# First stage of a decoder step: memory keys and values as plain fp32 products, and GpSimd's arithmetic given to VectorE and ScalarE

## The chip, the cores and the metric

The kernel runs on one core of a Trainium2 chip. The metric is the device time of one execution in microseconds (us), lower is better. A core has five engines, each with its own queue of instructions that it works off in order: TensorE (PE in the profile, its weight loads PEld), VectorE (DVE), ScalarE (ACT), GpSimd (POOL) and SyncE (SP, here only for transfers). They wait for each other by semaphores.

## The reference, cut to what matters

The reference is one inference step of a two-layer decoder over 256 prompt tokens and 8 x 8 sampled tokens, with 1024 features. Layer 0 is a state-space layer (S5), layer 1 latent attention; after each of them the tokens attend to 256 memory tokens and go through an MLP. What the change touches:

```python
def mem_kv(mem, g, w_k, w_v):          # once per layer; layer 0 is changed
    mn = rms_norm(mem, g)              # 256 memory rows x 1024
    k = mn @ w_k                       # 1024 x 1024, four heads of 256
    v = mn @ w_v
    return k, v                        # both are outputs too

def s5_mixer(u, a, dt, b, c, d_skip, w_glu, h0):   # layer 0, shortened
    # abar = exp(a dt); bbar = coef * b  (complex, 64 groups x 64 states)
    # state:  h[t] = abar h[t-1] + bbar u[t]   (per group of 16 channels)
    # output: y[t] = Re(c h[t]) + d_skip u[t]
    z = gelu(y) @ w_glu                # 1024 x 2048
    return z[..., :dm] * sigmoid(z[..., dm:])
```

## The kernel before, in words

**Stages.** The work goes stage by stage: the S5 layer with the memory keys and values of layer 0 beside it (to about 190 us), the GLU product (to about 266 us), the memory attention and MLP of layer 0, and then layer 1 in the same way. The change is in the first stage alone.

**Split products.** Products with weights are made in three parts (`mm3`, lines 194 to 198). A weight chunk of 128x1024 is loaded (`wraw`); ScalarE makes its rounded high part (`whi`, line 190), and VectorE or, for the chunk numbers in `POOL_LO`, GpSimd makes the rest (`wlo`, line 191). The other operand is split in the same way, into `mnh` and `mnl` for the memory rows. TensorE then multiplies high by high, high by low and low by high (L196, L197, L198). In the first stage there are two buffers each for raw, high and low parts, so that at most two loads are under way.

**Memory keys and values** (`mem_kv`). Eight blocks of 256 columns, four of keys and four of values; each takes two chunks of weights, and each chunk 8 x 3 products of 128x128 by 256. VectorE multiplies a block of keys with the row norms (`kt`, L565), TensorE transposes it (`kps`), and ScalarE copies it out.

**S5.** The input `xc` is multiplied with its norms into `xr` (four times, L781), transposed (`ups`) and kept as `U`. `state_side(hq)`, for the four quarters hq, makes for each half hh the products of B with powers of a: `rb` from QX (L862), `t1` from QY (L863), their sum (L864). These tiles are called `tq` in the profile and share three buffers (tag `tmp4`). TensorE transposes `rb` (`rps`), ScalarE copies it to `rt`, and TensorE makes the states of each chunk (`sps`, L877). `out_side(hq)` makes the products of C with powers: `ca` from X1 (L900), `ct` from Y1 (L901), their sum (L902); for hq = 2 the tile is called `hca`. `scan(f)`, for both halves f of the groups, carries the states over the chunks in VectorE steps `sc` and `H` (L938 to L944) and copies them to `HS` (L959, L961). `outputs(hq)` uses `HS`, `ca` and `U` for the outputs (`yps`, `ytp`), whose split goes into the GLU.

**Order.** The program is written stage by stage, but the order on each engine is set when it is built, by a scheduler that simulates the program's times (`schedule_with_timeline_sim`, L1776). So other work brings another order, on other engines too. On the chip each engine keeps that order.

Of the kernel before, what the change touches and what calls it, by code (L numbers as in the profile page):

```python
# [10 lines left out]
F32 = mybir.dt.float32  # L11
# [73 lines left out]
POOL_LO = (3, 5) + (101,) + (102,) + (103,)  # L85
# [3 lines left out]
class Trunk:  # L89
# [17 lines left out]
    # statistics over the partitions of several feature blocks  # L107
# [24 lines left out]
    def root_ahead(self, extra=None):  # L132
        """the summand of a root to come, as a root itself: the function's table is loaded ahead"""
        b = self.sm.tile([128, 1], F32, name="rb", bufs=2)
        with self.tc.issue_after(self.last_exp.ins):
            self.nc.scalar.activation(b, self.eps[:, 1:2] if extra is None else self.eps[:, 2:3], AF.Sqrt)
        return b

    def exp_ahead(self):
        """the function's table is loaded ahead"""  # L140
        b = self.sm.tile([128, 1], F32, name="rb", bufs=2)
        with self.tc.issue_after(self.gate.ins):
            self.nc.scalar.activation(b, self.eps[:, 2:3], AF.Exp)

    def root(self, ss, dim, extra=None, tag="r", bias=None):
        """sqrt(ss / dim + eps) (or + extra)"""
# [24 lines left out]
    def wtile(self, kind, dtype):  # L171
        """a buffer for weights; the pools take turns"""
# [5 lines left out]
    def load_chunk(self, srcs, cols):  # L178
        """srcs: list of (column slice or AP shaper, dram AP); returns hi, lo [128, cols]"""
# [13 lines left out]

    def mm3(self, ps, wh, wl, xh, xl, start, stop):
# [5 lines left out]
    def dense(self, W, KT, nb, xh, xl, evac, Gs, n=NT, pairs=None, then=None, korder=None):  # L200
        """W: dram [KT*128, nb*128]; xh, xl: k -> AP [128, n]; Gs: group sizes.
        pairs: second column offset (in columns) for a group made of two halves."""
# [3 lines left out]
        while b0 < nb:  # L206
# [5 lines left out]
            for k0 in ks:  # L212
# [10 lines left out]
                # with the last weights a block is finished before the next  # L223
# [17 lines left out]
    def update(self, y, rt, gpost, stat=True):  # L241
        """h += y / rt * gpost"""
# [12 lines left out]
    def update_scaled(self, y, rt, gpost, gpre, restore=True):  # L255
        """h += y / rt * gpost; the next input is the split of (rt h) gpre for the new h, and its
        root takes eps rt^2: the factor rt of a token goes with the token's norm"""
# [28 lines left out]
    def next_root(self):  # L286
        """the root of the input that update_scaled left, once it is needed"""
        st, ex = self.pending
        return self.root(self.stat_sum(st), D, extra=ex)
# [129 lines left out]
    def token_rows(self, row, name):  # L419
        """a row over the tokens [.., NT] by blocks of tokens: [128, 3]"""  # L420
# [5 lines left out]
    def h_to_tokens(self, s, rt):  # L426
        """the residual s / rt with the tokens on the partitions"""
# [12 lines left out]
    def finish(self, W, KT, fh, fl, y, gpost, ex):  # L440
        """the last product, norm and residual: the norm with the tokens on the partitions"""
# [55 lines left out]
    def mem_x(self, pool):  # L497
# [8 lines left out]
    def mem_root(self):  # L506
        """the norms of the rows of the memory: in the first layer they go with the products"""
# [15 lines left out]
    def mem_prepare(self, l, mp, x):  # L523
# [3 lines left out]
        for j in range(KD):  # L527
            ps = (self.ps_at if l else self.ps_mm).tile([128, 512], F32, name="mps", tag="at" if l else "mm")
            for i in range(2):
# [3 lines left out]
            nc.vector.scalar_tensor_tensor(xl[:, j, :], m, g(j), xh[:, j, :].bitcast(F32),  # L533
                                           op0=ALU.mult, op1=ALU.subtract)
        self.kt = mp.tile([128, KD, MT], F32, name="kt", tag="kt")

    def mem_kv(self, l, op, x):
        """in units: the keys (two blocks of features each), then the values (a head each)"""
# [5 lines left out]
        for g in range(8):  # L544
            W, c0 = (Wk, g * 256) if g < 4 else (Wv, (g - 4) * 256)
            ps = [self.ps_mm.tile([128, 512], F32, name="mm", tag="mm") for _ in range(2)]
            for k0 in range(0, KD, 4):
                hi, lo = self.load_chunk([(lambda t: t.rearrange("p (k c) -> p k c", c=256), W[:, k0:k0 + 4, c0:c0 + 256])], 1024)
# [40 lines left out]
    def s5(self, mkv):  # L589
        sp, close_sp = self.open("s5")  # L590
        mn, close_mn = self.open("memn0", side="right")
        mx = self.mem_x(mn)
# [43 lines left out]
    def s5_scan(self, sp, mkv, mx):  # L636
# [5 lines left out]
        # parameters, rows: group; the state index twice  # L642
# [15 lines left out]
        # B and C, rows: (real | imaginary part, group)  # L658
# [10 lines left out]
        # rows: (half of the features, chunk)  # L669
# [7 lines left out]
        # the gains of the layer's input go into B and the skip weights  # L677
        nc.gpsimd.tensor_mul(nat['b'][:, :K * N].rearrange("p (k n) -> p n k", k=K),
# [3 lines left out]
        nc.gpsimd.tensor_mul(dn, dn, gxn[:G])  # L682
# [22 lines left out]
        # r of the tokens, rows: (half of the features, chunk), columns: steps  # L705
# [23 lines left out]
        # coefficients  # L729
# [14 lines left out]
        # products with a power, rows: (real | imaginary part)  # L744
        #   state side, descending powers times the coefficient: re x (qr | qi) + im x (-qi | qr)
        #   output side, powers 1..8: re x (pr | -pi) + im x (-pi | -pr)
# [20 lines left out]
        for t, v in ((X1, PI), (Y1, PR)):  # L767
            nc.gpsimd.tensor_scalar(t[bot], v[bot], -1.0, None, op0=ALU.mult)
        self.mem_root()
        self.chunk = 100  # L770
        self.mem_gains(sp)
        # chunks: rows (step, channel), one block of columns per group
# [6 lines left out]
        for fb in range(4):  # L779
            xr = xp.tile([2 * NCH, 8, L, K], F32, name="xr", bufs=2)  # L780
            nc.gpsimd.tensor_mul(xr, xc[:, :, fb * 128:(fb + 1) * 128].rearrange("p s (g k) -> p g s k", k=K),  # L781
# [10 lines left out]
        # B and C, rows: the state index twice  # L792
# [30 lines left out]
        # a^8, a^16, .. a^128 by (half of the groups, state index), with the signs of the complex product  # L823
# [16 lines left out]
        # states at the start of each chunk (H) and after the last (F), rows: (half of the groups, state index)  # L840
# [15 lines left out]
        def state_side(hq):  # L856
            rt = self.xp.tile([128, 2, 8, 128], F32, name="rt", tag="xl" if hq % 2 else "xh", padded_shape=[128, 2, 10, 128])
            for hh in range(2):
# [4 lines left out]
                (V if hq < 2 else nc.gpsimd).tensor_mul(t1, b4(BI, gs), p4(QY, gs))  # L863
# [21 lines left out]
        def out_side(hq):  # L885
            ca = []
            E = nc.gpsimd
# [15 lines left out]
            # impulse responses, rows: input channel  # L903
# [20 lines left out]
        # states after each chunk: a scan by doubling, up and down, over 16 columns of groups  # L924
        def scan(f):
# [24 lines left out]
            # the states by (real | imaginary part, state index)  # L950
# [62 lines left out]
        if True:  # L1013
            # final states
# [43 lines left out]
    def kv_open(self, l, kvp):  # L1058
        """keys and values of the sample group, loaded ahead"""
# [29 lines left out]
    def mem_attention(self, l):  # L1089
# [8 lines left out]
        if True:  # L1098
# [35 lines left out]
            # the softmax scales of the rows: prompt tokens (two blocks), sample rows (head, sequence, step)  # L1134
# [10 lines left out]
            # sample group  # L1145
# [42 lines left out]
            # prompt group  # L1188
# [68 lines left out]
    def mlp(self, l):  # L1257
# [5 lines left out]
        with tc.tile_pool(name="mlp", bufs=1, reuse_waits="tile") as hp:  # L1263
            # y = r^2 y' with y' the product without r: the post norm takes y' with eps / r^4
# [32 lines left out]
    def mla(self, close_mn):  # L1297
# [7 lines left out]
        if True:  # L1305
# [23 lines left out]
            if True:  # L1329
# [15 lines left out]
                # latent and rotary key  # L1345
# [18 lines left out]
                # rotary key on both halves of the partitions  # L1364
# [32 lines left out]
                # queries  # L1397
# [21 lines left out]
                # the prompt group takes keys and values out of the latent, the sample group its queries into it  # L1419
# [71 lines left out]
                def values_of(half):  # L1491
                    """the values of four heads"""
# [287 lines left out]
```

## Time and profile before

| what | value |
|---|---|
| time, median of 3 runs | 1270.54 us (1269.88 to 1273.55) |
| span of the profiled execution, first to last instruction | 1267.7 us |
| TensorE busy, share of the span | 1136.2 us, 90% |
| VectorE busy | 774.2 us, 61% |
| ScalarE busy | 560.1 us, 44% |
| GpSimd busy | 269.4 us, 21% |
| chain that ended last, by engine | PE 73%, DVE 16%, DMA 3%, ACT 2%, POOL 2% |
| mean granted TensorE clock | 0.956 |

The times are of executions without a profile; the span is of one profiled execution, and the difference between it and the median is 2.8 us. The shares are means over the span. They hide that the stages have different limits, so the change has to be read from its own stage: the stretches and single rows below.

### The profile page before, as it was taken

How to read it: one execution, taken by the hardware profiler on the slowest of the kernel's cores; microseconds unless marked ns; L12 is line 12 of the kernel's file. 1: busy time of each engine (PE TensorE's matmuls, PEld its weight loads, DVE VectorE, ACT ScalarE, POOL GpSimd, SP SyncE). 2: the span in 40 equal slices, each digit the busy share in tenths (PEclk: the TensorE clock that was granted, in tenths of full speed). 3: DMA queues.
4: the chain of work that ended last, by engine and by line, in shares of the span. 5: the costliest groups of instructions: out<-in, count | busy, mean ns of one | idle time of the engine just before them, and what ended most of it. 6: DMA issues, size and time to landing. Idle time of an engine off the chain costs nothing.

```text
span 1267.7 us, 21389 instructions
## 1 busy us (share of the span) xinstructions
PE 1136.2 (90%) x8233; PEld 1030.5 (81%) x8233; DVE 774.2 (61%) x1253; ACT 560.1 (44%) x1006; POOL 269.4 (21%) x229
## 2 busy tenths in 40 slices
PE   3665579989998899999999999999899989999996
PEld 2564568988687899999988996559776989999996
DVE  5999994467447763355478586334953495435543
ACT  5434346444344453355356435223533455434531
POOL 3656430035003500000031034400620050000011
PEclk9877789999998999999999999998899989999998
DMA  7221446863733254444443554626454324544441
GB/s 148 75 92 46 103 72 170 296 247 128 271 130 119 74 182 150 136 156 157 151 150 111 167 179 142 201 71 249 151 199 167 116 84 134 165 150 150 149 138 55
DMA packets 151234, 184.86 MB, mean 146 GB/s; under 512 B 16719, under 2 KB 119388, under 8 KB 151068
## 3 DMA queue, kind: packets, MB, share of 16 engines
q1 hardware_dynamic: 141660, 174.84, 43.6%
q10 hardware_dynamic: 6976, 5.46, 1.4%
q0 software_dynamic: 2496, 3.20, 0.8%
q8 instruction: 65, 1.06, 0.3%
q14 instruction: 37, 0.30, 0.1%
HBM read 174.89 MB, written 6.21 MB: 143 GB/s over the span
## 4 chain that ended last, share of the span: by engine, by line
PE 73%; DVE 16%; DMA 3%; issue 2%; ACT 2%; POOL 2%; SPq 1%; POOLq 0%; DVEq 0%; ACTq 0%
PE mm L197 18%; PE mm L196 18%; PE mm L198 17%; DVE wlo L191 2%; PE kt L102 2%; PE sps L1159 2%; PE s L1639 2%; DVE sc L939 2%; DMA xc<-in_x_sample 1%; PE pov L1216 1%; PE ops L1174 1%; PE s L1680 1%; DVE H L944 1%; DVE xl L271 1%; PE pps L1194 1%
## 5 line engine op out<-in xcount | busy, mean ns | idle before, releaser
L191 DVE TENSOR_TENSOR wlo<-wraw,whi 128x1024 fp32r<-128x1024 f32 (+1 forms) x219 | 273.4, 1252 | 276.3 <-ACT whi L190 274.4
L190 ACT ACTIVATE whi<-wraw 128x1024 fp32r<-128x1024 f32 (+1 forms) x232 | 241.5, 1045 | 299.2 <-PE mm L197 250.1
L197 PE MATMUL mm<-xl,whi 128*128 128x320 f32 x944 | 295.9, 316 | 14.4 <-DVE xl L97 6.1
L196 PE MATMUL mm<-xh,whi 128*128 128x320 f32 x944 | 281.6, 318 | 8.4 <-ACT t_up L1272 3.7
L198 PE MATMUL mm<-xh,wlo 128*128 128x320 f32 x944 | 285.9, 313 | 1.9 <-DVE wlo L191 1.9
L197 PEld LDWEIGHTS mm<-xl,whi 128*128 128x128 f32 x944 | 181.0, 192 | 18.6 <-DVE xl L271 7.8
L196 PEld LDWEIGHTS mm<-xh,whi 128*128 128x128 f32 x944 | 176.5, 192 | 11.6 <-ACT t_up L1272 3.9
L198 PEld LDWEIGHTS mm<-xh,wlo 128*128 128x128 f32 x944 | 178.6, 192 | 2.3 <-DVE wlo L191 2.3
L196 PE MATMUL mm<-hh,whi 128*128 128x320 f32 x512 | 158.2, 309 | 0.0
L197 PE MATMUL mm<-hl,whi 128*128 128x320 f32 x512 | 158.0, 309 | 0.0
L198 PE MATMUL mm<-hh,wlo 128*128 128x320 f32 x512 | 157.1, 308 | 0.0
L191 POOL TENSOR_TENSOR wlo<-wraw,whi 128x1024 fp32r<-128x1024 f32 x13 | 32.4, 2493 | 304.7 <-ACT whi L190 216.7
L197 PEld LDWEIGHTS mm<-hl,whi 128*128 128x128 f32 x512 | 96.1, 188 | 0.0
L196 PEld LDWEIGHTS mm<-hh,whi 128*128 128x128 f32 x512 | 96.1, 188 | 0.0
L198 PEld LDWEIGHTS mm<-hh,wlo 128*128 128x128 f32 x512 | 95.9, 188 | 0.0
L118 POOL TENSOR_TENSOR sq<-sq 128x320 f32<-128x320 f32 x34 | 41.0, 1205 | 203.3 <-ACT sq L120 202.6
L248 POOL TENSOR_TENSOR t_up<-y,rr 128x320 f32<-128x320 f32 x6 | 7.5, 1258 | 218.3 <-DVE h L249 218.3
L102 PEld LDWEIGHTS kt<-ident,kn 128*128 128x128 f32 x256 | 30.1, 147 | 20.9 <-issue 5.8
L102 PE MATMUL kt<-ident,kn 128*128 128x128 f32 x256 | 39.2, 291 | 7.8 <-ACT ktb L1086 2.9
L102 PE MATMUL rps<-ident,tq 128*128 128x128 f32 x64 | 11.2, 324 | 37.1 <-DVE tq L864 26.1
L1568 POOL DMA_DIRECT2D rop<-in_cache_k_rope x64 | 34.4, 537 | 38.2 <-issue 20.5
L102 PEld LDWEIGHTS rps<-ident,tq 128*128 128x128 f32 x64 | 8.8, 167 | 37.8 <-issue 23.2
(483 smaller groups left out, 2171.4 us busy)
## 6 DMA issues: line engine op xcount, KB each, us to landing
wraw<-in_w_mlp_up SPq DMA_DIRECT2D x64, 512.0 KB, 3.9
wraw<-in_w_mlp_down SPq DMA_DIRECT2D x64, 512.0 KB, 3.6
kn<-in_cache_mem_k SPq DMA_DIRECT2D x16, 1024.0 KB, 7.6
vn<-in_cache_mem_v SPq DMA_DIRECT2D x16, 1024.0 KB, 9.4
wraw<-in_w_mem_k SPq DMA_DIRECT2D x16, 512.0 KB, 3.3
wraw<-in_w_mem_v SPq DMA_DIRECT2D x16, 512.0 KB, 3.8
wraw<-in_w_glu SPq DMA_DIRECT2D x32, 256.0 KB, 3.5
wraw<-in_w_mem_q SPq DMA_DIRECT2D x16, 512.0 KB, 4.0
```

The costliest lines, as they stand in the source:

```text
L102: self.nc.tensor.transpose(out, in_, self.ident[b:b + k, b:b + k])
L118: eng.tensor_add(st['acc'], st['acc'], st['last'])
L190: nc.scalar.activation(hi[:, :cols], raw[:, :cols], AF.Copy)
L191: (nc.gpsimd if self.chunk in POOL_LO else nc.vector).tensor_sub(lo[:, :cols], raw[:, :cols], hi[:, :cols].bitcast(F32))
L196: nc.tensor.matmul(ps, wh, xh, start=start, stop=False)
L197: nc.tensor.matmul(ps, wh, xl, start=False, stop=False)
L198: nc.tensor.matmul(ps, wl, xh, start=False, stop=stop)
L271: lo = nc.vector.scalar_tensor_tensor(xl[:, j, :], s, gpre(j), xh[:, j, :].bitcast(F32), op0=ALU.mult, op1=ALU.subtract)
L939: V.tensor_mul(m[1], swp, bc(a8i))
L1159: nc.tensor.matmul(sps[h * 32:(h + 1) * 32, :MT], qm[:, h * 2 + db, j * 128 + i * 32:j * 128 + (i + 1) * 32], ktb[:, h * 2 + db, :], start ...
L1568: last[eng] = eng.dma_start(dst, src[bass.ds(v, 1)].rearrange("o p d -> (o p) d"))
L1639: nc.tensor.matmul(s[o(b), :], ql(rb, b), lts[b][:, rb, :], start=rb == 0, stop=False, skip_group_check=True)
```

## The change

- The memory keys and values of layer 0 become plain fp32 products. The weights are not split; `load_plain` uses the six buffers of raw, high and low parts in turn, so that six loads may be under way. The memory rows are one tile, `mnp`, without a low part. A chunk takes 8 products in place of 24. Layer 1 keeps the split form.
- GpSimd's arithmetic in this stage goes to VectorE: the gains into B and into the skip weights (`natb`, `dn`), `xr`, `t1` of the quarters 2 and 3, and all of `out_side`.
- The negations for X1 and Y1 go from GpSimd to ScalarE.
- Comments are dropped, so that line numbers move by 22 or 23 in the functions below.

```diff
-POOL_LO = (3, 5) + (101,) + (102,) + (103,)
+POOL_LO = (3, 5)
...
+    def load_plain(self, src):
+        kind = ('raw', 'hi', 'lo')[self.plain % 3]
+        self.plain += 1
+        raw = self.wtile(kind, F32)
+        self.last_w = self.nc.sync.dma_start(raw.rearrange("p (k c) -> p k c", c=256), src)
+        return raw
...
-    def mem_x(self, pool):
+    def mem_x(self, pool, plain=False):
+        if plain:
+            return pool.tile([128, KD, MT], F32, name="mnp"), None
         return (pool.tile([128, KD, MT], F32R, name="mnh"), pool.tile([128, KD, MT], F32R, name="mnl"))
...
-            nc.vector.scalar_tensor_tensor(xl[:, j, :], m, g(j), xh[:, j, :].bitcast(F32),
-                                           op0=ALU.mult, op1=ALU.subtract)
+            if xl is not None:
+                nc.vector.scalar_tensor_tensor(xl[:, j, :], m, g(j), xh[:, j, :].bitcast(F32),
+                                               op0=ALU.mult, op1=ALU.subtract)
...
+                if xl is None:
+                    raw = self.load_plain(W[:, k0:k0 + 4, c0:c0 + 256])
+                    for kk in range(4):
+                        k = k0 + kk
+                        for b in range(2):
+                            w = raw[:, kk * 256:(kk + 1) * 256]
+                            bs = slice(b * 128, (b + 1) * 128)
+                            if g < 4:
+                                nc.tensor.matmul(ps[b][:, :MT], w[:, bs], xh[:, k, :], start=k == 0, stop=k == KD - 1)
+                            else:
+                                nc.tensor.matmul(ps[b][:, :256], xh[:, k, bs], w, start=k == 0, stop=k == KD - 1)
+                    continue
...
-        mx = self.mem_x(mn)
+        mx = self.mem_x(mn, plain=True)
...
-        nc.gpsimd.tensor_mul(nat['b'][:, :K * N].rearrange("p (k n) -> p n k", k=K),
+        V.tensor_mul(nat['b'][:, :K * N].rearrange("p (k n) -> p n k", k=K),
...
-        nc.gpsimd.tensor_mul(dn, dn, gxn[:G])
+        V.tensor_mul(dn, dn, gxn[:G])
...
-            nc.gpsimd.tensor_scalar(t[bot], v[bot], -1.0, None, op0=ALU.mult)
+            A.activation(t[bot], v[bot], AF.Copy, scale=-1.0)
         self.mem_root()
-        self.chunk = 100
+        self.plain = 0
...
-            nc.gpsimd.tensor_mul(xr, xc[:, :, fb * 128:(fb + 1) * 128].rearrange("p s (g k) -> p g s k", k=K),
+            V.tensor_mul(xr, xc[:, :, fb * 128:(fb + 1) * 128].rearrange("p s (g k) -> p g s k", k=K),
...
-                (V if hq < 2 else nc.gpsimd).tensor_mul(t1, b4(BI, gs), p4(QY, gs))
+                V.tensor_mul(t1, b4(BI, gs), p4(QY, gs))
...
-            E = nc.gpsimd
+            E = V
```

The order on the engines, at the three places of which the prediction speaks. In the new numbering L885 to L887 are QX, QY and their sum in `state_side`, L923 to L925 the three of `out_side`, L804 is `xr`, L588 `kt`, and L982 and L984 are the HS copies.

VectorE, at the first half-steps of `state_side`, before:

```order
L834 TENSOR_TENSOR a8r<-a8n 128x32
L863 TENSOR_TENSOR tq<-m_b,QY 128x1024
L862 TENSOR_TENSOR tq<-m_b,QX 128x1024
L832 TENSOR_TENSOR a8n<-a8r 128x32
L833 TENSOR_TENSOR a8n<-a8i 128x32
L835 SCALAR_TENSOR_TENSOR a8i<-a8r,a8i 128x32
L191 TENSOR_TENSOR wlo<-wraw,whi 128x1024
L864 TENSOR_TENSOR tq<-tq 128x1024
L565 TENSOR_TENSOR kt<-mm,rB 128x256 x2
L834 TENSOR_TENSOR a8r<-a8n 128x32
L191 TENSOR_TENSOR wlo<-wraw,whi 128x1024
L863 TENSOR_TENSOR tq<-m_b,QY 128x1024
```

The same place after:

```order
L857 TENSOR_TENSOR a8r<-a8n 128x32
L923 TENSOR_TENSOR hca<-m_c,X_211 128x8x128 x2
L804 TENSOR_TENSOR xr<-xc,rC 80x1024
L886 TENSOR_TENSOR tq<-m_b,QY 128x1024
L885 TENSOR_TENSOR tq<-m_b,QX 128x1024
L855 TENSOR_TENSOR a8n<-a8r 128x32
L856 TENSOR_TENSOR a8n<-a8i 128x32
L858 SCALAR_TENSOR_TENSOR a8i<-a8r,a8i 128x32
L588 TENSOR_TENSOR kt<-mm,rB 128x256
L804 TENSOR_TENSOR xr<-xc,rC 80x1024
L887 TENSOR_TENSOR tq<-tq 128x1024
L857 TENSOR_TENSOR a8r<-a8n 128x32
```

The low parts of weights between the half-steps are gone, and products of `out_side` and `xr` stand between them.

TensorE, at the first transposes of `rb` (`rps`), before:

```order
L198 MATMUL mm<-mnh,wlo 128x256
L102 MATMUL ups<-ident,xr 128x80 x16
L102 MATMUL rps<-ident,tq 128x128 x8
L102 MATMUL kps<-ident,kt 128x128 x2
L196 MATMUL mm<-mnh,whi 128x256
L197 MATMUL mm<-mnl,whi 128x256
```

The same place after (`whi` and `wlo` are here two of the buffers of plain weights):

```order
L567 MATMUL mm<-mnp,wraw 128x256
L102 MATMUL kps<-ident,kt 128x128 x2
L567 MATMUL mm<-mnp,whi 128x256 x8
L102 MATMUL ups<-ident,xr 128x80 x8
L567 MATMUL mm<-mnp,wlo 128x256 x8
L102 MATMUL ups<-ident,xr 128x80 x8
L102 MATMUL kps<-ident,kt 128x128 x2
L102 MATMUL rps<-ident,tq 128x128 x8
```

Whole chunks of plain products stand between the transposes of the input and ahead of the first `rps`.

VectorE, at the end of the second scan, before:

```order
L191 TENSOR_TENSOR wlo<-wraw,whi 128x1024
L942 TENSOR_TENSOR sc<-sc 128x16x15
L944 TENSOR_TENSOR H<-H,sc 128x2x8x15
L959 COPY HS<-H 64x16x32
L961 COPY HS<-H 64x16x32
L191 TENSOR_TENSOR wlo<-wraw,whi 128x1024
L918 TENSOR_TENSOR kk<-kk,dd 16x128 x2
L97 TENSOR_TENSOR xl<-gt,xh 128x320 x2
```

The same place after:

```order
L967 TENSOR_TENSOR H<-H,sc 128x2x8x7
L97 TENSOR_TENSOR xl<-gt,xh 128x320 x2
L965 TENSOR_TENSOR sc<-sc 128x16x15
...
L941 TENSOR_TENSOR kk<-kk,dd 16x128
L967 TENSOR_TENSOR H<-H,sc 128x2x8x15
L941 TENSOR_TENSOR kk<-kk,dd 16x128
L965 TENSOR_TENSOR sc<-sc 128x16x15
L191 TENSOR_TENSOR wlo<-wraw,whi 128x1024
L967 TENSOR_TENSOR H<-H,sc 128x2x8x15
L982 COPY HS<-H 64x16x32
L984 COPY HS<-H 64x16x32
```

The split of the outputs (`xl`) and the additions to `kk` stand ahead of the HS copies now, and the copies end the row. On TensorE the same shift puts 48 products of the GLU ahead of the outputs of the third quarter (`yps<-hca`), where 6 stood.

## Rows read from the trace of the kernel before

**Rows 1.** The page, the span in 40 slices: busy tenths of VectorE.

```profile
DVE  5999994467447763355478586334953495435543
```

**Rows 2.** Stretches: busy of PE, PEld, DVE, ACT, POOL; clock; DMA share, GB/s.

```profile
26.00:40.00 14.00, 10.25 (x53) 8.92 (x54) 13.76 (x27) 10.98 (x24) 5.17 (x3) 1.00 0.29 93
40.00:180.00 140.00, 88.86 (x982) 81.01 (x980) 138.66 (x211) 59.58 (x123) 79.11 (x35) 0.82 0.29 77
...
220.00:266.00 46.00, 44.06 (x312) 43.56 (x311) 20.63 (x26) 20.14 (x33) 0.00 (x0) 1.00 0.91 318
```

**Rows 3.** ScalarE in order of time: start, duration, instruction, wait before it.

```profile
23.52 0.63 ACT L709 ACTIVATE sq<-xc 80x512 f32<-80x512 f32 x1 [6.42 <-DMA xc<-in_x_sample]
```

**Rows 4.** GpSimd by line and form, 0 to 230 us: count, busy, mean.

```profile
L901 POOL TENSOR_TENSOR ct<-m_c,Y 128x1024 f32<-128x1024 f32 x8 | 17.4, 2175 | 0.5
L902 POOL TENSOR_TENSOR ca<-ca,ct 128x1024 f32<-128x1024 f32 x6 | 16.2, 2692 | 0.2
L900 POOL TENSOR_TENSOR ca<-m_c,X 128x1024 f32<-128x1024 f32 x6 | 14.3, 2404 | 20.2 <-PE yps L978 20.2
L781 POOL TENSOR_TENSOR xr<-xc,rC 80x1024 f32<-80x1024 f32 x4 | 8.6, 2170 | 1.0 <-POOL X L768 1.0
L863 POOL TENSOR_TENSOR tq<-m_b,QY 128x1024 f32<-128x1024 f32 x4 | 7.9, 1981 | 30.8 <-DVE tq L864 30.8
L191 POOL TENSOR_TENSOR wlo<-wraw,whi 128x1024 fp32r<-128x1024 f32 x3 | 7.2, 2400 | 24.2 <-ACT whi L190 24.2
L900 POOL TENSOR_TENSOR hca<-m_c,X 128x1024 f32<-128x1024 f32 x2 | 4.8, 2414 | 0.0
L902 POOL TENSOR_TENSOR hca<-hca,ct 128x1024 f32<-128x1024 f32 x2 | 4.7, 2368 | 0.2
```

**Rows 5.** VectorE in order of time, columns as in group 3.

```profile
43.71 1.07 DVE L760 TENSOR_TENSOR QX<-T,T 128x512 f32<-128x512 f32 x1
...
53.60 5.83 DVE L763 TENSOR_TENSOR QY<-T,T 128x512 f32<-128x512 f32 x1
...
59.65 1.59 DVE L834 TENSOR_TENSOR a8r<-a8n 128x32 f32<-128x32 f32 x1
...
87.72 1.21 DVE L191 TENSOR_TENSOR wlo<-wraw,whi 128x1024 fp32r<-128x1024 f32 x1
...
133.26 2.36 DVE L939 TENSOR_TENSOR sc<-H,a8i 128x16 f32<-128x16 f32 x1
...
140.10 0.17 DVE L939 TENSOR_TENSOR sc<-H,a8i 128x16 f32<-128x16 f32 x1
...
175.60 2.36 DVE L942 TENSOR_TENSOR sc<-sc 128x32 f32<-128x32 f32 x1
...
189.14 0.42 DVE L961 COPY HS<-H 64x512 f32<-64x512 f32 x1
```

**Rows 6.** GpSimd in order of time, beside group 5.

```profile
133.16 2.43 POOL L902 TENSOR_TENSOR ca<-ca,ct 128x1024 f32<-128x1024 f32 x1
...
175.53 2.38 POOL L902 TENSOR_TENSOR ca<-ca,ct 128x1024 f32<-128x1024 f32 x1
```

**Rows 7.** One line of VectorE: shortest, median and longest in ns.

```profile
L862 DVE TENSOR_TENSOR tq<-m_b,QX x8: 1206/1210/3042, 48.3 to 127.4; 128x1024 f32<-128x1024 f32 x8
```

**Rows 8.** TensorE in order of time: split products of the memory keys.

```profile
34.73 0.41 PE L198 MATMUL mm<-mnh,wlo 128*128 128x256 f32 x1
34.94 0.41 PE L196 MATMUL mm<-mnh,whi 128*128 128x256 f32 x1
...
85.96 0.28 PE L198 MATMUL mm<-mnh,wlo 128*128 128x256 f32 x1
...
86.91 0.28 PE L197 MATMUL mm<-mnl,whi 128*128 128x256 f32 x1
```

**Rows 9.** Chain of waits, 262 to 268 us, then 352 to 358 us.

```profile
266.26 0.15 PE mm L197
...
354.31 1.74 PE pps L1194 x8
```

## The prediction

> **What bounds the kernel now.** I read the page's slices first. VectorE is at nine tenths from the second to the sixth slice, so (at 31.7 us a slice) from 32 to 190 us, and nowhere else for as long [rows 1]. The busy time by stretch says the same with numbers: from 40 to 180 us VectorE works 138.66 of 140 us, TensorE 88.86 at a mean clock of 0.82, ScalarE 59.58, GpSimd 79.11, and the DMA engines have a share of 0.29 [rows 2]. ScalarE, transfers and GpSimd have air; VectorE has none. Up to about 26 us the program waits for its first input: ScalarE idles 6.42 us for xc and goes on at 23.52 [rows 3]. The stage in which VectorE is the bound ends with the last copy of the second half's states (HS), at 189.14 + 0.42 = 189.56 us [rows 5]. After that TensorE has the path: in 220 to 266 us it works 44.06 of 46 us [rows 2], and the chain there is a row of split products [rows 9].
>
> The next question is why VectorE needs 163.5 us (189.5 less 26). One by one its rows show the reason. The scan's product on 128x16 takes 0.17 us at 140.10, and 2.36 us at 133.26 [rows 5]; beside the long one GpSimd adds two blocks of 1024 elements, from 133.16 for 2.43 us [rows 6]. Both end together. The last of this kind, at 175.60, again lies on a GpSimd row that begins at 175.53 and is as long [rows 5, 6]. Of the products on QX the shortest takes 1206 ns, the median 1210, the longest 3042 [rows 7]. QY takes 5.83 us where its twin QX takes 1.07 [rows 5]. In this way 28 VectorE instructions, the first at 59.65 and the last at 175.60 [rows 5], are over half a microsecond longer than the shortest of the same line and shape, 52 us in all, and five more (QY the longest) than a neighbour of the same size, 12 us: 64 us by 33 instructions.
>
> **The change part by part.** *GpSimd's work goes away.* Its eight forms are 35 instructions of 81.1 us [rows 4], 32 of which are given to VectorE (the other three are low parts of weights, which nobody makes any more). If they stop VectorE as rows 5 to 7 show, 64 us go. The lower bound is the 52 us of the 28; the upper is the whole 81.1.
>
> The skill states a stricter rule (the Trainium skill, "SBUF — State Buffer", section "Who interferes with whom"): a VectorE instruction with two SBUF inputs contends with a GpSimd instruction that reads SBUF, and whoever issues first holds the shared port for its whole length. By it all 81.1 us stand in VectorE's way; the rows agree on the kind and give 64 of it, since VectorE also does work with one input meanwhile. By the rule the sum below would be 17 us better.
>
> *VectorE gets work.* 32 instructions of 1024 elements at 1.21 us (the undisturbed price of the same size, [rows 5, 7]): +38.7. The split of the memory weights goes: 13 low parts on VectorE at 1.21 [rows 5]: −15.7. In the new order three more low parts of the GLU's weights stand before the last states (the third pair of excerpts shows one of them): +3.6. The gains into B and the skip weights (natb, dn) come on top, eight low parts of the memory's rows go; at most 1.2 us each way, and natb stands before 26 us, under the wait for xc: nothing. ScalarE loses 16 copies and gets two negations; with 59.58 of 140 us it hides that.
>
> So VectorE's own work is 163.5 − 64 − 15.7 + 38.7 + 3.6 = 126.1 us, 37.4 less.
>
> *TensorE gets longer products.* Eight split products follow each other in 0.95 us, 0.119 each, at full clock, and at 0.21 early on [rows 8]. A plain product shows in another stage: eight records, two for each of four products of 128x128 by 256, in 1.74 us, so 0.435 each [rows 9]. The 128 plain products cost 55.7 us, the 384 split ones 45.7: +9.9, and +28.5 where the clock is half. This is 1.22 times the three reduced products. The skill (the Trainium skill, "FP8 and Floating Point Precision", section "TensorE Precision Notes") has four passes through the array for true fp32, which is 1.33 times and would be 61 us: a rule against the change; row and rule differ by 5 us of TensorE time, and the row is for this shape.
>
> *Where VectorE then waits for TensorE.* The work of both shrinks from 163.5 us towards 126, with more on TensorE, so the cover gets thin. t1 and rb share three buffers; a half-step's t1 takes the buffer of the rb before it, and this comes free only when TensorE has transposed it. TensorE's order puts 75 plain products before the end of the fourth half-step's transposes. From 34.73 us [rows 8]: 75 x 0.435 = 32.6, over a clock of 0.82 [rows 2] 39.8; some 112 transposes and small products, estimated at 0.119 each, 13.3: 88 us. VectorE, its rows added up in the new order, would be there at about 83. That is a stall of 5. Three others, walked in the same way (the first keys, and two later half-steps), come to some 4. I take 9; the bounds are 0 (higher clock once TensorE works without gaps) and 33 (half the clock through the 128 products, +28.5, and these four).
> Behind the waiting instruction in VectorE's queue stand the scan of the first half, and behind that all outputs; nothing passes it. Gain so far 37.4 − 9 = 28.4.
>
> *The tail.* In the new order 48 GLU products stand before the outputs of the third quarter, 6 before. 42 at 0.147 (the spacing in the chain, [rows 9]) are 6.2 us that come out of the row after the states, if their weights are there. But 220 to 266 us moves 318 GB/s at a share of 0.91 [rows 2], close to what the queues give. I count three quarters: 4.6; bounds 0 and 6.2.
>
> Sum: 28.4 + 4.6 = 33 us. The profiled execution spans 1267.7 us; 2.8 us lie between that and the median of 1270.54. 1267.7 − 33 + 2.8 = 1237.5; I say 1238. Everything after the GLU has nearly the same order, so I carry the gain to the end.
>
> **The rivals.** *TensorE becomes the bound of a part.* The stage would be some 130 us long. TensorE's 88.86 + 10.25 us of 26 to 180 [rows 2] and 9.9 to 28.5 more are 109 to 128. That is for it; against it, its busy time counts the 0.28 to 0.41 us of each pipelined product although they follow at 0.119 to 0.21 [rows 8]. The stalls would then be 17 to 38 in place of 9, the gain 4 to 25: 1246 to 1267. Chance 0.23.
>
> *The whole of GpSimd's time was in VectorE's way, and nothing stalls.* 37.4 + 9 to 17 and the whole tail: a gain of 46 to 60, 1211 to 1224. For it speak the equal ends of rows 5 and 6; against it, that VectorE's stretched rows make 64. The skill's exclusive port (the page on SBUF) would have this one. Chance 0.09.
>
> *Slower: TensorE at half clock up to the second scan.* All 128 plain products at 0.87 are 111 us, and some 20 us of other work 40: keys and values end at about 34.7 + 151 = 186 less what follows, roughly 177, not about 110. The second scan needs state products that stand behind them on TensorE, and takes some 47 us from there with the copies: 224 us, against 189.5, so +35: 1305. It decides from the point where about 45% of TensorE's work runs at the lower level. For it: the clock was 0.82 on the mean already, with gaps. Against it: longer products leave fewer gaps. Chance 0.06.
>
> *The change does not do what it says* (the wait for buffers gives all of it back): 0.04, no change.
>
> **How the numbers follow.** My forecast, a gain of 25 to 46, 1224 to 1246, has 0.58. Below are 0.09, above 0.23 + 0.04 + 0.06. A range of 1222 to 1260 leaves out about half of the case below, a third of the TensorE case, and the last one: near 0.2. A change of 0.3% (3.8 us) is what a measurement of this kernel can tell from none. Faster: 0.58 + 0.09 + 0.23 = 0.90; same 0.04; slower 0.06.
>
> **What would show it.** VectorE rows of 1024 elements at 1.2 us and no scan row of over a microsecond between 40 us and the last HS copies; those copies end at about 156 to 162 us. GpSimd has next to no work there. Plain products follow at 0.435, or 0.87 where the clock is half. The GLU ends at about 233 us, and later stages lie the same 33 us earlier. I am wrong if VectorE shows idle time of over 15 us on TensorE's transposes, if the long rows stay although GpSimd rests, or if the stages after the GLU stretch.

## The result and the profile after

The changed kernel takes 1231.22 us (median of 4 runs, 1229.15 to 1235.15) against 1270.21 before: a ratio of 0.9694, 95% interval 0.9671 to 0.9718, so 39 us less. The profiled execution is the slowest of the four; its span is 1233.5 us.

The page's slices and the stretches of the changed kernel, columns as in [rows 1, 2]; below them the lines of the kernel before for the two same parts of the program (up to the end of the HS copies, and from there up to the end of the GLU's products):

```profile
DVE  5998944664468553564587674416843685435543
POOL 2000000350027000000050054202700140000011
```

```profile
26.00:40.00 14.00, 11.65 (x54) 9.39 (x53) 13.47 (x35) 9.11 (x21) 0.00 (x0) 0.87 0.71 239
...
158.06:229.45 71.39, 68.07 (x538) 66.03 (x537) 26.77 (x39) 34.06 (x57) 1.80 (x1) 0.98 0.75 241
26.00:158.06 132.06, 110.46 (x981) 94.29 (x979) 121.35 (x293) 61.76 (x140) 0.00 (x0) 0.91 0.46 116
```

```profile
26.00:189.56 163.56, 101.89 (x1043) 92.27 (x1044) 161.87 (x271) 71.41 (x147) 84.28 (x37) 0.83 0.30 76
189.56:268.16 78.60, 75.50 (x613) 72.42 (x612) 33.04 (x48) 41.40 (x70) 1.81 (x1) 0.97 0.82 260
```

VectorE's row of nines ends one slice earlier and has an eight in it, and GpSimd rests after its first memsets. From 26 us to the last HS copy the stage takes 132.06 us, not 163.56: VectorE works 40.5 us less, and idles 10.7 us instead of 1.7. TensorE works 8.6 us more in 31.5 us less, at a clock of 0.91 instead of 0.83. The 0.83 seems too high: [rows 2] give 1.00 for 26 to 40 us, but up to 37 us the split products of the kernel before follow each other at 0.21 us, and from there on at 0.12, as later at full clock [rows 8]:

```profile
36.44 0.41 PE L197 MATMUL mm<-mnl,whi 128*128 128x256 f32 x1
36.65 0.41 PE L198 MATMUL mm<-mnh,wlo 128*128 128x256 f32 x1
...
37.04 0.28 PE L197 MATMUL mm<-mnl,whi 128*128 128x256 f32 x1
37.16 0.28 PE L198 MATMUL mm<-mnh,wlo 128*128 128x256 f32 x1
```

With 11 us at half clock the mean is 0.79 by estimate.

VectorE of the changed kernel in order of time, with the idle time before a row in brackets; then one line of it (shortest, median, longest in ns), which answers to [rows 7]:

```profile
88.31 1.23 DVE L923 TENSOR_TENSOR ca<-m_c,X 128x1024 f32<-128x1024 f32 x1 [1.97 <-PE h0ps L102]
...
123.48 1.23 DVE L191 TENSOR_TENSOR wlo<-wraw,whi 128x1024 fp32r<-128x1024 f32 x1 [3.11 <-ACT whi L190]
...
157.63 0.42 DVE L984 COPY HS<-H 64x512 f32<-64x512 f32 x1
```

```profile
L885 DVE TENSOR_TENSOR tq<-m_b,QX x8: 1203/1222/1230, 45.4 to 100.9; 128x1024 f32<-128x1024 f32 x8
```

The longest product on QX was 3042 ns and is 1230. Of the 28 rows that were over half a microsecond longer than a twin (52 us) none is left. The HS copies end at 158.05.

TensorE at the plain products, early and a little later, and the GLU's end (a row of xN has N records; two records are one plain product):

```profile
26.39 2.04 PE L567 MATMUL mm<-mnp,wraw 128*128 128x256 f32 x4
...
48.98 2.32 PE L567 MATMUL mm<-mnp,whi 128*128 128x256 f32 x10
...
229.30 0.31 PE L206 MATMUL mm<-xh,wlo 128*128 128x320 f32 x1
229.45 0.70 PE L128 MATMUL ss<-sq,ones 128*128 128x320 f32 x2
```

The same place of the kernel before:

```profile
268.16 0.70 PE L128 MATMUL ss<-sq,ones 128*128 128x320 f32 x2
```

With 0.379 us for the last record, ten records in 2.32 us follow at 0.216, so a plain product takes 0.43; four in 2.04 (the last one 0.763) give 0.85 at the low clock (0.50 granted from 26 to 28 us). The first plain product starts at 26.39; the first split one of the kernel before at 29.15, and not at 34.73, where the rows that were read begin [rows 8]. After the GLU's products TensorE makes the sums of squares `ss`: at 229.45, in the kernel before at 268.16. The GLU thus ends 38.7 us earlier. In the kernel before the products still run behind the row of [rows 9] at 266.26, so the tail from HS to there was 78.6 us, and is 71.4. The rest of the program, from there to the end, took 999.5 us before and 1004.0 in this profile; in a second profile of the same changed kernel (x9 below; GLU end at 227.28) 1000.6. Over all the profiles of this case whose later stages are the same program it is 995.6 to 1005.2, so the 4.5 us are within the scatter of the later stages.

### The profile page after: what moved, and what is told of

The parts are those of the page before. It is cut to its first block, busy times and chain, and to the rows that moved or that the text cites. A ratio compares the mean times of both kernels' runs of the same rounds, so it can differ in the third digit from the quotient of the medians.

```text
span 1233.5 us, 21037 instructions
## 1 busy us (share of the span) xinstructions
PE 1139.3 (92%) x8105; PEld 1026.6 (83%) x8105; DVE 726.7 (59%) x1266; ACT 546.7 (44%) x992; POOL 182.3 (15%) x190
## 4 chain that ended last, share of the span: by engine, by line
PE 75%; DVE 10%; DMA 5%; SPq 3%; issue 2%; ACT 2%; POOL 2%; POOLq 0%; DVEq 0%; ACTq 0%
PE mm L205 17%; PE mm L204 17%; PE mm L206 17%; PE kt L102 2%; PE sps L1182 2%; PE mm L567 2%; DVE xl L279 2%; PE s L1662 2%; SPq L944 2%; DVE wlo L191 1%; DMA natc<-in_ssm_c_im 1%; PE pov L1239 1%; PE s L1703 1%; PE pps L1217 1%; PE mm L569 1%
## 5 line engine op out<-in xcount | busy, mean ns | idle before, releaser
L191 DVE TENSOR_TENSOR wlo<-wraw,whi 128x1024 fp32r<-128x1024 f32 (+1 forms) x206 | 252.9, 1232 | 279.3 <-ACT whi L190 269.1
L190 ACT ACTIVATE whi<-wraw 128x1024 fp32r<-128x1024 f32 (+1 forms) x216 | 224.5, 1044 | 302.8 <-PE mm L205 246.6
L191 POOL TENSOR_TENSOR wlo<-wraw,whi 128x1024 fp32r<-128x1024 f32 x10 | 25.4, 2538 | 286.4 <-ACT whi L190 198.1
L1591 POOL DMA_DIRECT2D rop<-in_cache_k_rope x64 | 34.5, 540 | 37.4 <-issue 20.4
L1107 DVE COPY ktb<-kt 128x512 f32<-128x512 f32 x32 | 22.0, 687 | 21.0 <-PE kt L102 20.9
L1109 ACT ACTIVATE ktb<-kt 128x512 f32<-128x512 f32 x32 | 19.1, 596 | 31.4 <-PE kt L102 26.0
```

The source lines that it names most:

```text
L190: nc.scalar.activation(hi[:, :cols], raw[:, :cols], AF.Copy)
L191: (nc.gpsimd if self.chunk in POOL_LO else nc.vector).tensor_sub(lo[:, :cols], raw[:, :cols], hi[:, :cols].bitcast(F32))
L1591: last[eng] = eng.dma_start(dst, src[bass.ds(v, 1)].rearrange("o p d -> (o p) d"))
```

## The experiments

Each was timed against the kernel before on the same chip; the medians of the latter are 1270.1 to 1270.7 us throughout, so that the runs can be compared with each other too. Where a line number stands in an excerpt it is that of the experiment's own code.

**Only the move (x1_move_only).** The memory keys and values go back to the split form, all low parts on VectorE.

```diff
-        mx = self.mem_x(mn, plain=True)
+        mx = self.mem_x(mn)
-        self.plain = 0
+        self.chunk = 100
```

> Only GpSimd's work is moved (to VectorE and ScalarE); the memory keys and values keep the split form, all their low parts on VectorE. Theory (GpSimd's stops of 64 us and VectorE's own work add up): VectorE's stage is 163.5 - 64 + 38.7 for the moved work + 3.6 for three more low parts = 142 us, with 5 to 9 us of waits HS ends at about 175: a gain of 12 to 22 us, 1248 to 1258. Rival (the plain products with six loads in flight make the gain, the move only evens out): under 8 us, above 1262. Rival (the move makes all of it): 1240 or less.

Measured: 1243.44 us, ratio 0.9791 (0.9770 to 0.9811), 27 us less than before. Its stage up to the last HS copy, and from there to the end of the GLU:

```profile
26.00:170.28 144.28, 108.04 (x1107) 98.74 (x1106) 140.44 (x318) 77.60 (x160) 0.00 (x0) 0.86 0.41 103
170.28:241.05 70.77, 67.37 (x544) 64.89 (x544) 29.21 (x42) 34.11 (x58) 1.81 (x1) 1.00 0.80 250
```

VectorE works 140.44 us where the sum gave 142, and waits under 4. The time is better than the theory's 1248 because those waits are shorter than I put them and the tail is 8 us shorter here too. The larger part of the change's gain is GpSimd's silence.

**Only the plain products (x2_plain_only).** GpSimd keeps its work (`xr`, `t1` of two quarters, `out_side`, the gains, the negations).

```diff
-            E = V
+            E = nc.gpsimd
-                V.tensor_mul(t1, b4(BI, gs), p4(QY, gs))
+                (V if hq < 2 else nc.gpsimd).tensor_mul(t1, b4(BI, gs), p4(QY, gs))
...
```

> Only the memory keys and values are plain; GpSimd keeps all its work except the three low parts. Theory: VectorE loses 15.7 us of low parts and the stops by three GpSimd rows (about 6), the other stops stay, so 1.9 us rows are still there by the two dozen: a gain of 15 to 25 us, 1245 to 1256. Rival (plain products feed TensorE so much better that they make it all): 1240 or less. Rival (TensorE's longer products eat the gain): above 1262.

Measured: 1267.72 us, ratio 0.9969 (0.9947 to 0.9990): some 3 us, where the theory wanted 15 to 25. VectorE works only 137.24 us from 26 us to the last HS copy at 187.35, 24.6 less than before, but it idles 24.1 us instead of 1.7. The long rows stay: from 26 us on 30 rows are over half a microsecond longer than the shortest of their line and shape, by 55 us; counted in the same way, the kernel before has 30 with 56. What VectorE waited for (total, times, longest), and its two long waits for the states:

```profile
DVE sc L961 <- ACT H L904: 17.7, 3, 11.3
DVE natc L704 <- DMA natc<-in_ssm_c_im: 8.8, 1, 8.8
```

```profile
106.01 0.43 DVE L961 TENSOR_TENSOR sc<-H,a8r 128x256 f32<-128x256 f32 x1 [5.70 <-ACT H L904]
...
162.28 0.42 DVE L961 TENSOR_TENSOR sc<-H,a8r 128x256 f32<-128x256 f32 x1 [11.32 <-ACT H L904]
```

The engines that these waits lead to, in order of time: TensorE, ScalarE, and SyncE's queue:

```profile
96.92 6.21 PE L569 MATMUL mm<-wlo,mnp 128*128 128x256 f32 x16
...
149.89 2.42 PE L569 MATMUL mm<-whi,mnp 128*128 128x256 f32 x10
...
154.40 2.06 PE L900 MATMUL sps<-U,rt 128*64 128x40 f32 x60
```

```profile
104.65 0.39 ACT L904 ACTIVATE H<-sps 128x256 f32<-128x256 f32 x1 [5.33 <-PE sps L900]
...
159.59 1.06 ACT L190 ACTIVATE whi<-wraw 128x1024 fp32r<-128x1024 f32 x1 [7.20 <-DMA wraw<-in_w_glu]
...
161.47 0.39 ACT L904 ACTIVATE H<-sps 128x256 f32<-128x256 f32 x1 [0.46 <-ACT kvo L597]
```

```profile
148.32 6.04 SPq L944 DMA_DIRECT2D tt<-kk  x8
154.46 1.04 SPq L183 DMA_DIRECT2D wraw<-in_w_glu  x2
```

Read backwards, the first wait (5.70 us) ends with the products that make the states (`sps`); on TensorE they stand behind plain products that run at a granted clock of 0.57 (90 to 104 us), after 12.0 us in which TensorE waited for `kt` from VectorE. The second (11.32 us, from 150.95) has two parts. Up to 156.46 plain products and then the states' own products run on TensorE. From there the copies H stand in ScalarE's queue behind a split of GLU weights, which were asked for at 154.46, behind the stores of impulse responses in SyncE's queue. Of the 8.8 us for `natc` 3.4 lie behind 26 us. So my theory failed because it counted VectorE's work and not the queues of the others: TensorE with its plain products first, then a transfer that is not needed yet, which holds the queue of an engine whose next instruction is. This is read from the rows; no run takes one of these waits out. What it shows of the two parts: alone they give 27 and 3 us, together 39.

**Where GpSimd's stops come from (x3, x4, x12).** To the changed kernel, 24 or 48 GpSimd instructions are added, whose result nobody reads. The output is the same.

```diff
+                if hq == 0 and hh == 0:
+                    dm = s8.tile([128, 8, L, K], F32, name="dm", bufs=1)
+                    for _ in range(24):
+                        nc.gpsimd.tensor_mul(dm, b4(CR, gs), q4(X1, gs))     # x3
...
+                        nc.gpsimd.memset(dm, 0.0)            # x4: 48, behind one such product
...
+                        nc.gpsimd.tensor_copy(dm, U[:, :1024])               # x12: 24
```

> The changed kernel with 24 added GpSimd products of 128x1024 with two inputs, whose result nobody reads (about 50 us of GpSimd, from 50 us on). Theory (the two engines stop each other): VectorE's rows beside them are 1.9 us longer or wait as much, and HS ends 25 to 45 us later: 1255 to 1278. Rival (GpSimd was slow work that VectorE waited for by data, and did not stop it): under 5 us, below 1237.

> The changed kernel with 48 added GpSimd memsets of 128x1024 behind one product, so GpSimd is as busy but reads nothing. Theory (what stops VectorE is GpSimd's reading beside two inputs of VectorE): within 4 us of the changed kernel, and VectorE's 1024-element rows stay at 1.2 us. Rival (any work of GpSimd stops it): 25 us or more slower.

> The changed kernel with 24 added GpSimd copies of 128x1024, one input, read from U, nobody reads the result. Theory (GpSimd's reading is enough to stop a VectorE instruction with two inputs): VectorE's rows beside them are stretched as with the two-input products, 10 to 45 us slower by the copies' length. Rival (only GpSimd's two-input work stops it): within 5 us, as with the memsets.

Measured: 1271.18 us for two inputs (40 more than the changed kernel), 1235.14 for the memsets (1229.58 to 1240.56, 4 more by the medians, within their scatter), 1247.97 for one input (17 more). GpSimd's row of each (count, busy, mean in ns), one fence for each:

```profile
L929 POOL TENSOR_TENSOR dm<-m_c,X 128x1024 f32<-128x1024 f32 x24 | 79.9, 3329 | 41.7 <-DVE a8r L857 39.9
```

```profile
L930 POOL MEMSET dm<- 128x1024 f32 x48 | 45.7, 952 | 2.8
```

```profile
L929 POOL COPY dm<-U 128x1024 f32<-128x1024 f32 x24 | 46.2, 1924 | 54.0 <-ACT U L811 52.6
```

And VectorE's rows at the start of the 24 products of x3, with GpSimd's first four in the fence behind:

```profile
50.86 1.22 DVE L886 TENSOR_TENSOR tq<-m_b,QY 128x1024 f32<-128x1024 f32 x1
51.99 1.22 DVE L885 TENSOR_TENSOR tq<-m_b,QX 128x1024 f32<-128x1024 f32 x1
53.13 2.04 DVE L855 TENSOR_TENSOR a8n<-a8r 128x32 f32<-128x32 f32 x1
55.09 0.18 DVE L856 TENSOR_TENSOR a8n<-a8i 128x32 f32<-128x32 f32 x1
```

```profile
47.69 21.95 POOL L929 TENSOR_TENSOR dm<-m_c,X 128x1024 f32<-128x1024 f32 x4 [39.93 <-DVE a8r L857]
```

In x3 exactly 24 VectorE rows are over half a microsecond too long, by 43.0 us together: 1.8 us for each GpSimd product. In x12 it is 23 rows and 19.0 us, 0.83 each. With the 48 memsets it is 3 rows and 3.3 us: one beside the product in front, and two copies beside memsets. GpSimd's memsets at that place, and VectorE's rows:

```profile
92.49 1.96 POOL L930 MEMSET dm<- 128x1024 f32 x2
```

```profile
91.50 1.21 DVE L923 TENSOR_TENSOR ca<-m_c,X 128x1024 f32<-128x1024 f32 x1
92.63 0.89 DVE L987 COPY HS<-H 64x128 f32<-64x128 f32 x1
93.55 0.98 DVE L989 COPY HS<-H 64x128 f32<-64x128 f32 x1
```

In the changed kernel the two copies take 0.21 and 0.23 us; a third copy beside the memsets (`a8r` at 67.60) takes 0.69 instead of 0.24. All three end 0.08 us behind the end of a memset. The time follows: 40, 17 and some 4 us. So one GpSimd instruction that reads stops VectorE once. A GpSimd instruction that only writes stops none of VectorE's rows with two inputs here, but it does stop its copies, and there were only three of these. The kernel's own GpSimd work was paid in the same coin: 35 instructions, 33 long rows (that of QY holds more than one stop), and 64 us, 1.83 each.

GpSimd's busy time is larger than the stops: 79.9 against 43.0 us. Its four products from 47.69 take 21.95 us, 5.5 each (the shortest of the 24 takes 2.07), while VectorE's rows at 50.86 and 51.99 run undisturbed. So it waits too, and the profile books that as busy.

**The stores of impulse responses on GpSimd's queue (x5_tt_pool_queue).**

```diff
-                nc.sync.dma_start(tt[s * K:(s + 1) * K, s:], kk[:, 0:L - s])
+                nc.gpsimd.dma_start(tt[s * K:(s + 1) * K, s:], kk[:, 0:L - s])
```

> The changed kernel with the 32 stores of the impulse responses (kk to tt) issued by GpSimd's queue, where nothing else runs, in place of SyncE's. In the changed kernel these stores hold SyncE's queue while they wait for kk, and the GLU's weights behind them land late: ScalarE waits 4.93 and 5.50 us for them and VectorE 3.11 behind it. Theory (that wait is on the path): 3 to 9 us faster than the changed kernel, 1222 to 1228. Rival (GpSimd's queue takes longer to start a store, the outputs wait for tt): 2 us or more slower than the changed kernel. Second rival: same, the weights have slack.

Measured: 1234.92 us (1227.80 to 1237.78), ratio 0.9701 (0.9653 to 0.9748): no gain over the changed kernel, where the theory wanted 3 to 9 us. HS ends at 155.39, 2.7 us earlier, and the GLU at 230.27, 0.8 later. But the run did not take out the wait that it was made for; ScalarE's and VectorE's rows there:

```profile
119.55 1.06 ACT L190 ACTIVATE whi<-wraw 128x1024 fp32r<-128x1024 f32 x1 [6.38 <-DMA wraw<-in_w_glu]
```

```profile
120.64 1.23 DVE L191 TENSOR_TENSOR wlo<-wraw,whi 128x1024 fp32r<-128x1024 f32 x1 [5.89 <-ACT whi L190]
```

These GLU weights are asked for at 110.43, not at 118.53, yet the split starts only 2.8 us earlier, and its wait is 6.38 us where it was 5.50; VectorE's behind it is 5.89 where it was 3.11. What went is the 3.3 us of waits for copies of `kk`, whose additions now stand partly behind HS. Whether the wait for the weights is on the path thus stays open.

**Two loads in flight (x6_two_buffers).**

```diff
-        kind = ('raw', 'hi', 'lo')[self.plain % 3]
+        kind = 'raw'
```

> The changed kernel whose plain weights use the two raw buffers alone, so two loads in flight, not six. Theory (VectorE is the bound, two loads of 3.3 to 3.8 us keep up with 3.5 us of products a chunk): 0 to 6 us slower than the changed kernel, 1231 to 1237. Rival (that TensorE ran dense and at a high clock up to 86 us is owed to the six buffers): 10 us or more slower, with a clock near 0.83 again.

Measured: 1228.14 us (1226.32 to 1229.53), 3 us below the theory's range, clock 0.93 up to the last HS copy. The rival falls: TensorE's dense work does not need six buffers. Whether two are better stays with the last pair below.

**Twice the products (x7_double_products).**

```diff
+                                for d in range(2):
...
-                                nc.tensor.matmul(ps[b][:, :MT], w[:, bs], xh[:, k, :], start=k == 0, stop=k == KD - 1)
+                                    nc.tensor.matmul(ps[b][:, :MT], w[:, bs], xh[:, k, :], start=k == 0 and d == 0, stop=k == KD - 1 and d == 1)
```

> The changed kernel with each plain product of layer 0's memory keys and values made twice into the same sum, so they come out doubled: 128 more products of 0.435 us, 55.7 us of TensorE. TensorE is busy for 57.4 of 60 us from 26 to 86 in the changed kernel. Theory (TensorE is just short of the bound there): 25 to 50 us slower, 1256 to 1281, and VectorE waits for rps transposes. Rival (VectorE alone bounds, TensorE has room later): under 8 us slower.

Measured: 1267.30 us, ratio 0.9961 (0.9936 to 0.9987), 36 more than the changed kernel for 55.7 us of TensorE. The stretches, and the last group of value products:

```profile
60.00:100.00 40.00, 39.56 (x361) 34.29 (x360) 38.20 (x58) 17.66 (x45) 0.00 (x0) 1.00 0.33 69
100.00:143.00 43.00, 43.00 (x479) 35.49 (x478) 42.86 (x159) 18.65 (x41) 0.00 (x0) 1.00 0.38 77
143.00:180.00 37.00, 34.33 (x259) 29.89 (x258) 6.81 (x18) 12.73 (x27) 1.80 (x1) 0.95 0.38 74
180.00:220.00 40.00, 37.97 (x209) 34.77 (x208) 8.76 (x9) 13.55 (x20) 0.00 (x0) 0.96 0.54 168
```

```profile
L571 PE MATMUL mm<-wraw,mnp x96: 379/379/483, 121.6 to 198.3; 128*128 128x256 f32 x96
```

The size is as the theory has it, the place is not. HS ends at 143.48, 14.6 us earlier than in the changed kernel, because the new order lets the value products stand later, up to 198 us, between the outputs and ahead of the GLU. There TensorE has the path. VectorE's waits for the transposes of `rb`, which I expected, are not there. From 26 us to the end of the GLU TensorE had about 20 us of room (55.7 less 36): it idles 7.6 us instead of 24.9, and its mean clock there is 0.98 instead of 0.93. The HS copies alone do not tell how the stage stands.

**Layer 1 plain as well (x8_layer1_plain).**

```diff
-            x1 = self.mem_x(mn)
+            x1 = self.mem_x(mn, plain=True)
```

> The changed kernel with layer 1's memory keys and values plain as well. Theory (where TensorE has the path, the plain form costs what its products cost more, 128 x 0.435 - 384 x 0.119 = 9.9 us): 6 to 13 us slower, 1237 to 1244. Rival (the split's 16 low parts on VectorE and 16 high parts on ScalarE were in the way there too): same or faster.

Measured: 1235.95 us (1234.29 to 1240.72), ratio 0.9738 (0.9700 to 0.9777), 4.7 over the changed kernel by the medians. From the end of the GLU to the end it takes 1006.2 us, against 1004.0 and 1000.6 in the two profiles of the changed kernel. Slower, at about half the middle of the expected range and below its lower end; with the scatter of these stages (995.6 to 1005.2 without this edit) it is not settled more closely.

**More work off VectorE (x9 to x11).** The changed kernel again, then with `xr` on ScalarE, then with two buffers on top.

```diff
-            V.tensor_mul(xr, xc[:, :, fb * 128:(fb + 1) * 128].rearrange("p s (g k) -> p g s k", k=K),
-                                 rC[:, None, :, None].to_broadcast([2 * NCH, 8, L, K]))
+            for s in range(L):
+                A.activation(xr[:, :, s, :], xc[:, s, fb * 128:(fb + 1) * 128].rearrange("p (g k) -> p g k", k=K),
+                             AF.Copy, scale=rC[:, s:s + 1])
```

> The changed kernel once more, as the measure for the next two on the same chip: 1229 to 1235 us.

> The changed kernel with the four xr products made by ScalarE, in 32 pieces of 80x128 with a scale for each row, in place of four VectorE products of 1.2 us. Theory (VectorE is still the bound of the stage): 4.9 us less of VectorE, ScalarE has 62 of 132 us busy and takes some 8 us more beside it: 3 to 6 us faster than the changed kernel. Rival (TensorE, which the doubled products showed to be just short of the bound, takes over): within 2 us of it.

> The same with the plain weights in the two raw buffers alone. With two buffers the changed kernel had 1228.1 against 1231.2, within their scatter. Theory (two loads in flight are enough, and the first loads are disturbed less): 0 to 4 us faster than the run with xr on ScalarE alone, 1222 to 1229. Rival (that was scatter): same as it within 1 us.

Measured: 1231.24 us (ratio 0.9697, 0.9675 to 0.9718) for the changed kernel again; 1221.46 (0.9621, 0.9597 to 0.9646) with `xr` on ScalarE; 1224.55 (0.9634, 0.9614 to 0.9655) with two buffers too. With `xr` on ScalarE, up to the last HS copy:

```profile
26.00:151.79 125.79, 110.81 (x987) 94.62 (x987) 117.56 (x290) 72.91 (x173) 0.00 (x0) 0.93 0.50 123
```

```profile
L805 ACT ACTIVATE xr<-xc,rC 80x128 f32<-80x128 f32 x32 | 9.7, 388 | 1.3 <-DVE rC L737 1.2
```

9.7 us of ScalarE replace 4.8 of VectorE, and the kernel is 9.8 us faster than the changed one, better than both kernels. VectorE's work is 3.8 us less than in the changed kernel and its idle time 2.5 less, and the GLU ends at 220.93, 8.5 earlier than in the first profile and 6.4 than in the second. This is more than the 3 to 6 us forecast. How much of the surplus is the new order of the queues I did not separate; the later stages are also the shortest of all profiles here (995.6 us), which is scatter by what was said above. The two buffers gave 3 us less in one pair and 3 us more in the other; as an effect of their own they do not show, and the 0 to 4 us forecast for them in the last run did not come.

## Why the prediction was right, point by point

- **VectorE was the bound, and GpSimd's stops were the larger part.** Right. The sum gave 37.4 us less work on VectorE; the trace shows 161.87 − 121.35 = 40.5. GpSimd's term holds by x1 (140.44 us against 142 by the same sum), and its kind and the price of one stop by x3, x4 and x12.
- **64 us rather than 81.** Right, and x3 says why: by the busy time it would be 79.9 us, the stops are 43.0. The Trainium skill ("SBUF — State Buffer", "Who interferes with whom") has the engine that comes second fully blocked, and a GpSimd instruction that only writes free of contention with a VectorE instruction of two inputs; x4 agrees, and x12 agrees on the reading. The prediction's estimate by that rule took GpSimd's busy time for the length of its instructions, although this time holds its own waits. The reason that the prediction gave for the difference, VectorE's work with one input, is not what these rows show.
- **Price of a plain product.** 0.435 us forecast, 0.43 measured at full clock, 0.85 against 0.87 at the low one.
- **Where VectorE waits for TensorE: this step failed.** The size was near (9 us forecast; the idle time rose from 1.7 to 10.7), the place was wrong. For the transposes of `rb` VectorE waits 0.5 us in all. I let TensorE start its keys at 34.73 us and run at the clock of before (0.82); it starts at 26.39, where the kernel before started at 29.15, and from 26 to 86 us, the stretch that I walked, the clock was 0.95. The waits stand elsewhere: 3.9 us for high parts of GLU weights, 3.3 for copies of `kk`, 2.0 for the transposes of the cached states. So the 9 us came out by luck.
- **HS copies end at 156 to 162 us:** 158.05. **Tail:** 4.6 us forecast, 7.2 measured (9.7 in the second profile), over my upper bound of 6.2. TensorE works 68.07 us there instead of 75.50. The bound rested on 42 products only; the split of the outputs and the additions to `kk` went ahead of HS too. No run separates these, and the tail is as short in x1 (70.77). I also took about 266 us for the GLU's end, which is 268.16.
- **The time.** 33 us forecast, 39.0 between the medians: 3.1 more in the stage (31.5 for 28.4), 2.6 in the tail, and the rest scatter. The two profiled executions themselves differ by 34.2 us, since in the later one the stages behind the GLU happen to be 4.5 us longer.
- **The rivals.** TensorE as bound of a part, and the slower case, did not come: from 60 to 100 us TensorE works 39.75 of 40 us at a granted clock of 1.00, where it worked 24.97 at 0.83. The margin is some 20 us of TensorE's time (x7). In x2 a piece of these rivals is there: plain products at 0.57, and the scan behind them. That the whole of GpSimd's 81 us would go did not come either.

## What to carry to other kernels

Where VectorE is the bound, look for its rows that are a microsecond or two longer than their twins: each reading GpSimd instruction beside them stopped it once here, for a little less than the shortest such GpSimd row (1.8 us by 2.07 with two inputs, 0.83 by 1.04 with one), so work that VectorE does in 1.2 us is cheaper there, and here cheaper still on ScalarE (x10). Leaving out work on the bound engine pays only as far as the in-order queues of the others (plain products ahead of the states, a split that waits for its weights) let the next work come in time: one part of the change gave 3 us alone, and 12 behind the other.

## What was not expected of the hardware

- A GpSimd product whose shortest row is 2.07 us takes 5.5 on the mean of four beside VectorE rows that follow without a gap, and these stay at 1.2; then a small row (0.18 us undisturbed) takes 2.04 us. Either engine can be the late one.
- Memsets of GpSimd, which leave VectorE's products at 1.2 us, hold its copies: 0.89 and 0.98 us in x4 where the changed kernel has 0.21 and 0.23.
- TensorE's clock rose with the change, from 0.83 (0.79 by the estimate above) to 0.91 up to the HS copies, and to 1.00 from 60 to 143 us with twice the products, where TensorE works 82.56 of 83 us, although each product is longer.
